# Seven block products in ten more pairs of tiles: the second halves of both gates and the output projection in 1024-column groups

## The chip, the cores and the metric

One NeuronCore of a Trainium2 chip runs the whole program. The metric is the device time of one execution in microseconds (us). A kernel is given by the median of its runs; a profiled execution also has a trace, and the trace's span is a little shorter than the time of the execution it belongs to.

## The reference

One layer (DEPTH 1) on 256 positions of width 2048, float32. Cut to what matters here:

```python
def mixer_block(x, g_norm, w_in, ln_g, ln_b, w_s, b_s, rpb, w_branch, w_out):
    h = rms_norm(x, g_norm)
    proj = h @ w_in                                   # 2048 -> 9216 columns
    uv, qkv, gates = jnp.split(proj, [2 * GM_WIDTH, 2 * GM_WIDTH + 3 * NA_WIDTH], axis=-1)
    q, k, v = jnp.split(qkv, 3, axis=-1)
    y_a = gmlp_branch(uv, ln_g, ln_b, w_s, b_s)       # 256 x 1024
    y_b = neighbourhood_attn(q, k, v, rpb)            # 256 x 1024
    g_a, g_b = jnp.split(jax.nn.sigmoid(gates), 2, axis=-1)   # 2048 columns each
    merged = g_a * (y_a @ w_branch[:GM_WIDTH]) + g_b * (y_b @ w_branch[GM_WIDTH:])
    return x + merged @ w_out                         # 2048 -> 2048

def conv_ffn(x, g_norm, w_up, conv_k, conv_b, w_down):
    up = rms_norm(x, g_norm) @ w_up                   # 2048 -> 2 * 5504
    ...                                               # depthwise convolution of width 3
    return x + (jax.nn.silu(gate) * val) @ w_down     # 5504 -> 2048
```

A final RMSNorm follows. Nearly all of the arithmetic is in the five matrix products with `w_in`, `w_branch`, `w_out`, `w_up` and `w_down`.

## The kernel before, in words

Every float32 operand of a matrix product is split into a high part of type fp32r and the low remainder, and each product is three matmuls: high by high, low by high, high by low (`three_products`, L365, its matmuls L368 to L370). The activations are split once; the weights are split as they arrive.

**The stream of weights.** `weight_stream` (L54) lists all products as groups of pieces of 128 x 1024 numbers (512 KB). The order of this list is the order of the program. For each piece `begin` (L340) first issues loads on the SP queue (`load`, L217; five raw buffers `wraw`), then prepares pieces up to four ahead (`prepare`, L336): ScalarE (ACT) writes the high part (`high`, L249), VectorE (DVE) the low part (`low`, L252) into a pair of tiles called a unit (`whi`, `wlo`). There are four units, and two more from the output projection on. Then the tasks that earlier steps put down for this piece run (`at`, `run_tasks`), and then TensorE (PE) gets the piece's matmuls. All engines work through their own queue in the order of the program.

**The kinds of group.** A `nat` group (`nat_step`, L394) has 512 output columns; a piece holds two input tiles of 128, and for each of the two blocks of 128 positions there are 2 x 3 matmuls into that block's PSUM bank: 12 matmuls a piece. The gates are four such groups of eight pieces for each half of the columns: `("gate", br, j)` for branch `br` 0 or 1 and column block `j` 0 to 3. The branch projections `("branch", br, j)` have four pieces each, the output projection `("out", j)` eight. A `ws` group keeps the weights in place (`u`, `q`, `k`, `up`). A `wide` group has 1024 output columns and one input tile a piece: 2 x 2 output blocks of 128 positions by 512 columns, 12 matmuls a piece, in four PSUM banks. The down projection is made of four wide groups (`wide_step`, L428).

**Seven block products.** In some pairs of neighbouring tiles of the down projection (`FF_SEVEN`) the 2 x 2 by 2 x 2 block product is done with seven block products in place of eight, in the manner of Strassen and Winograd. Such a pair takes 21 matmuls in place of 24 and uses seven banks, with the fourth output block eight, which is all of PSUM. For it the weights are prepared in three steps (`sums`, L286): `plain` splits one half block (the tile `half`) and one whole piece, `summed` makes four sums of 128 x 512 on DVE (L305 to L308) in the raw buffers and splits the first, `last` splits the second. That takes a half tile and three units for two pieces. The activations need four sums as well (`token_sums`). After the group's last such pair `combine` (L459) adds the extra banks to the output: ACT copies one bank (L464), DVE does the rest (L466, L467, and `rest`, L962), and the banks become free.

**Around the change.** The order is now: attention and the first gates; `branch` 0 and 1 for `j` 0 and 1; then for `j` 2 and 3 `gate(0, j)`, `gate(1, j)`, `branch(0, j)`, `branch(1, j)`; then `out` 0 to 3; then the first up group. `ev_gate` (L904) applies the sigmoid on ACT straight from PSUM. `ev_branch` (L913) multiplies the projection by its gate (L917) and adds the two branches (L921). `turn_m` (L925) transposes merged columns on PE (L935, eight transposes) two pieces later and splits them into the tiles `m` (L598, L603). `ev_out` (L971) adds the projection to `x2` (L968) and squares it on ACT; `turn_x2` (L988) transposes the result for the up projection (L995, L605). `open_x2` (L1232) gives the memory of the merge stage to `x2`, to the two more units and to the half tile, and loads `x` again on the POOL queue (L1239).

Of the kernel before, what the change touches and what calls it, by code (L numbers as in the profile page):

```python
# [48 lines left out]
FF_BLOCKS = ((0, 22), (22, 43))  # L49
FF_SEVEN = ((3, 5, 7), (2, 4, 6))  # L50
LAST = 4


def weight_stream():  # L54

    groups, order = {}, []

    def add(key, kind, w, pieces):
        groups[key] = (kind, w, pieces)
        order.extend([key] * len(pieces))
# [12 lines left out]

    def gate(br, j):  # L80
        nat(("gate", br, j), "w_in", 0, KD, (GA0, GB0)[br] + j * 512)

    def branch(br, j):
        nat(("branch", br, j), "w_branch", br * 8, 8, j * 512)

    add(("vg",), "wide", "w_in", [([k], (("x", T), (V0, 1024))) for k in range(KD)])
    for j in range(2):
        add(("u", j), "ws", "w_in", by_two(0, KD, (U0 + j * 512, 512)))
    for j in range(2):
        nat(("va", j), "w_in", 0, KD, VA0 + j * 512)  # L90
        qk(j)
    gate(0, 0)
    qk(2)
    gate(1, 0)
    qk(3)
    gate(0, 1)
    gate(1, 1)
    for j in range(2):
        branch(0, j)
        branch(1, j)  # L100
    for j in (2, 3):
        gate(0, j)
        gate(1, j)
        branch(0, j)
        branch(1, j)
    for j in range(4):
        nat(("out", j), "w_out", 0, KD, j * 512)
    for n, (f0, f1) in enumerate(FF_BLOCKS):
        for f in range(f0, f1, 2):
            nb = min(2, f1 - f) * 128  # L110
            add(("up", f), "ws", "w_up", by_two(0, KD, (f * 128, nb), (DFF + f * 128, nb)))
        for j in range(2):
            wide(("down", n, j), "w_down", j * 1024, down_tiles(n))
    return groups, order
# [38 lines left out]
def trunk_kernel(ctx, tc, x, weights, vectors, ln_g, ln_b, w_s_turned, b_s, rpb, norm_final, out):  # L153
# [46 lines left out]
    start_free = []  # L200
    unit_free = [(wpool, n) for n in range(UNITS[0])]
    half_free = []
    raw, units, halves = {}, {}, {}
    n_loaded = [0]
    tasks = {}
    preload = {}
# [31 lines left out]
    def unit(key, low_at=0):  # L238
# [3 lines left out]
        units[key] = (h, l, slot)  # L242
        return h, l

    def unit_done(key):
        unit_free.append(units.pop(key)[2])

    def high(h, w):
        nc.scalar.activation(h, w, AF.Copy)  # L249
# [175 lines left out]
                done(box["ps"], i + 1)  # L425
        return step

    def wide_step(key, acts, sevens, rest, done, by_block=0):  # L428


        n0, size = starts[key], size_of[key]
# [26 lines left out]

        def combine(i):  # L459

            nu, nv = (fx["p"].tile([128, 512], F32, name=f"comb{n}") for n in range(2))

            def one():
                nc.scalar.activation(nu, p(1), AF.Copy)  # L464
                rest(0, 0, nu, OP.add)
                nc.vector.tensor_sub(nu, nu, p(6))  # L466
                nc.vector.tensor_sub(nv, nu, p(7))  # L467
                free(p(1), p(6), p(7))

            def two():  # L470
                rest(0, 1, nu, OP.subtract)
                rest(0, 1, p(5), OP.add)
                rest(1, 0, nv, OP.add)

            def three():
                rest(1, 1, nv, OP.subtract)
                rest(1, 1, p(5), OP.add)
                free(p(5))

            for n, f in enumerate((one, two, three)):  # L480
                at(i + 3 if by_block else i + 1 + n, f)

# [420 lines left out]

    def ev_gate(br, j):  # L904
        def done(ps, i):
            g = mg["p"].tile([128, NT, 512], F32, name=f"g{br}", bufs=2)
# [3 lines left out]
            mg[br, j] = g  # L910
        return done

    def ev_branch(br, j):  # L913
        def done(ps, i):
            g = mg[br, j]
            for t in range(NT):
                nc.vector.tensor_mul(g[:, t, :], ps[t], g[:, t, :])  # L917
            free(*ps)
            if br == 1:
                for t in range(NT):  # L920
                    nc.vector.tensor_add(g[:, t, :], g[:, t, :], mg[0, j][:, t, :])  # L921
                at(i + 2, lambda: turn_m(j))
        return done

    def turn_m(j):  # L925
        if j == 0:
            mg["mp"], mg["m_st"] = pool("mT", "left")
            mg["mT"] = [mg["mp"].tile([128, 2, T], F32R, name=f"m{k}") for k in range(KD)]
        g = mg[1, j]
        for k2 in range(2):  # L930
            p = bank()
            for kk in range(2):
                c = k2 * 2 + kk
                for t in range(NT):
                    nc.tensor.transpose(p[:, kk * T + t * 128:kk * T + (t + 1) * 128],  # L935
                                        g[:, t, c * 128:(c + 1) * 128], ident)
            k = j * 4 + k2 * 2
            split_pair(p, mg["mT"][k:k + 2], None)
            free(p)

    def token_sums(f, s):

# [11 lines left out]


    rs = {}
    fx = {}

    def into_x2(j):
        def go(t, c, v, op):  # L960
# [20 lines left out]

    def norm2():
# [169 lines left out]
    for j in range(4):  # L1152
        steps["qk", j] = ws_step(("qk", j), xt, ev_qk(j))
        for br in range(2):
            steps["gate", br, j] = nat_step(("gate", br, j), xt, ev_gate(br, j))
            steps["branch", br, j] = nat_step(("branch", br, j), lambda k, br=br: yT[br * 8 + k], ev_branch(br, j))
    for n in range(len(FF_BLOCKS)):
# [3 lines left out]
    for j in range(4):  # L1161
        steps["out", j] = nat_step(("out", j), lambda k: mg["mT"][k], ev_out(j))
# [62 lines left out]
    def close_attention():  # L1225
        assert at_pool["done"] == HEADS // 2
        at_pool["st"].close()

    before["branch", 0, 1] = close_attention
    rs["ss"] = const.tile([128, NT, 4], F32, name="ss_2")  # L1230

    def open_x2():  # L1232
# [4 lines left out]
        rs["x2"] = xp.tile([128, NT, D], F32, name="x2")  # L1237
        for t in range(NT):
            nc.gpsimd.dma_start(rs["x2"][:, t, :], x[0, t * 128:(t + 1) * 128, :])  # L1239
        fx["p"], f_st = pool("seven", "right")  # L1240
        ctx.push(f_st)
        unit_free.extend((fx["p"], UNITS[0] + n) for n in range(UNITS[1]))
        half_free.extend((fx["p"], n) for n in range(HALVES))

    at(starts["out", 0] + 3, open_x2)

    def open_ff():
        mg["m_st"].close()
# [68 lines left out]
```

## Time and profile before

| | |
|---|---|
| median of three runs | 1321.99 us (1321.98 to 1323.04) |
| profiled execution | 1321.85 us, its span 1319.4 us |
| granted PE clock, mean | 0.997 |
| busy, PE / PE weight load / DVE / ACT / POOL | 1307.8 / 1114.7 / 945.5 / 728.8 / 100.1 us |
| branch 0 and 1, `j` = 1 | 356 to 378 us of the span |
| gates and branches, `j` = 2 and 3 | 378 to 511.6 us |
| output projection | 511.6 to 602.2 us |
| second part of the down projection, first group | 1198.5 to 1255 us |

The busy time of a group is the time in which at least one of its instructions ran. The matmuls are pipelined, so that the mean duration of one is longer than the distance from one to the next. A page of the profile gives shares over the whole span; the stretches in the table are the ones in which the changed work lies, or in which work of the same kind is done already.

### The profile page before, as it was taken

Reading aid. Unit: us, or ns where it says so; the run is one execution under the profiler, and the core shown is the slowest. Engines: PE = TensorE matmul, PEld = TensorE weight load, DVE = VectorE, ACT = ScalarE, POOL = GpSimd, SP = SyncE. Lnnn points to the kernel's source line nnn. Section 1 sums busy time; section 2 is a strip of 40 time slices with the busy share of each in tenths; the row PEclk is TensorE's granted clock in tenths of the full one; section 3 lists DMA queues with packets and bytes.
Section 4 is the critical chain, followed back from the end, with each engine's and each line's share of the span. In section 5 each row is a group of like instructions: output and inputs, shape, how many; then the busy total and the mean of one; then the engine's idle time right before and its main releaser. Section 6 shows DMA issues by size and latency. Waiting matters only on the chain.

```text
span 1319.4 us, 18485 instructions
## 1 busy us (share of the span) xinstructions
PE 1307.8 (99%) x6782; PEld 1114.7 (84%) x6782; DVE 945.5 (72%) x1362; ACT 728.8 (55%) x1072; POOL 100.1 (8%) x192
## 2 busy tenths in 40 slices
PE   9999999999999999999999999999999999999996
PEld 8888888888888888888888888888888888888885
DVE  6676667776564546565878777797858787869987
ACT  6755566676444444544655555554545555546553
POOL 0502075430000000000000000000000000000000
PEclk9999999999999999999999999999999999999998
DMA  9957676645556667665565656556655655546643
GB/s 349 316 170 213 202 207 196 202 156 184 188 188 187 194 188 259 196 201 182 179 203 176 196 178 202 178 169 229 209 190 191 192 187 197 180 140 223 235 164 128
DMA packets 74042, 261.40 MB, mean 198 GB/s; under 512 B 9568, under 2 KB 10720, under 8 KB 73440
## 3 DMA queue, kind: packets, MB, share of 16 engines
q1 hardware_dynamic: 69984, 252.46, 58.4%
q0 software_dynamic: 3680, 7.30, 2.1%
q8 instruction: 53, 0.87, 0.3%
q10 hardware_dynamic: 288, 0.47, 0.1%
q14 instruction: 37, 0.30, 0.1%
HBM read 256.00 MB, written 2.10 MB: 196 GB/s over the span
## 4 chain that ended last, share of the span: by engine, by line
PE 97%; DVE 2%; DMA 1%; ACT 0%; issue 0%; POOL 0%; DVEq 0%; ACTq 0%; POOLq 0%
PE bank L353 31%; PE bank L359 16%; PE bank L368 15%; PE bank L370 15%; PE bank L369 15%; PE bank L386 1%; PE bank L385 1%; PE bank L388 1%; DMA wraw<-in_weights_dram 1%; PE bank L834 1%; DVE wlo L252 0%; PE bank L886 0%; DVE x L962 0%; PE bank L565 0%; PE bank L708 0%; PE bank L995 0%
## 5 line engine op out<-in xcount | busy, mean ns | idle before, releaser
L252 DVE TENSOR_TENSOR wlo<-wraw,whi 128x1024 fp32r<-128x1024 f32 (+1 forms) x466 | 561.1, 1218 | 227.7 <-ACT whi L249 220.4
L249 ACT ACTIVATE whi<-wraw 128x1024 fp32r<-128x1024 f32 (+1 forms) x466 | 481.3, 1047 | 279.7 <-PE bank L369 162.4
L353 PE MATMUL bank<-h,whi 128*128 128x512 f32 x1760 | 426.2, 393 | 0.0
L353 PEld LDWEIGHTS bank<-h,whi 128*128 128x128 f32 x1760 | 321.7, 188 | 64.3
L359 PEld LDWEIGHTS bank<-h,wlo 128*128 128x128 f32 x1760 | 224.5, 188 | 9.8
L359 PE MATMUL bank<-h,wlo 128*128 128x256 f32 x1760 | 228.4, 281 | 0.0
L368 PE MATMUL bank<-whi,h 128*128 128x512 f32 x320 | 126.0, 394 | 0.0
L370 PE MATMUL bank<-wlo,h 128*128 128x512 f32 x320 | 124.7, 390 | 0.0
L369 PE MATMUL bank<-whi,h 128*128 128x512 f32 x320 | 124.6, 389 | 0.0
L370 PE MATMUL bank<-wlo,a 128*128 128x512 f32 x248 | 96.6, 389 | 0.0
L368 PE MATMUL bank<-whi,a 128*128 128x512 f32 x248 | 96.5, 389 | 0.0
L369 PE MATMUL bank<-whi,a 128*128 128x512 f32 x248 | 96.5, 389 | 0.0
L1024 ACT ACTIVATE tc<-ta,vec 128x256 f32<-128x256 f32 x86 | 47.0, 594 | 84.4 <-DVE ta L1022 84.4
L700 DVE TENSOR_TENSOR ta<-bank,tb 128x256 f32<-128x256 f32 x110 | 39.0, 417 | 67.1 <-ACT tb L698 67.1
L698 ACT ACTIVATE tb<-bank 128x256 f32<-128x256 f32 x110 | 36.2, 384 | 90.5 <-PE bank L353 85.7
L370 PEld LDWEIGHTS bank<-wlo,h 128*128 128x128 f32 x320 | 60.0, 188 | 12.7
L368 PEld LDWEIGHTS bank<-whi,h 128*128 128x128 f32 x320 | 60.1, 188 | 12.3
L369 PEld LDWEIGHTS bank<-whi,h 128*128 128x128 f32 x320 | 60.1, 188 | 12.0
L370 PEld LDWEIGHTS bank<-wlo,a 128*128 128x128 f32 x248 | 46.5, 188 | 9.9 <-DVE wlo L252 0.3
L369 PEld LDWEIGHTS bank<-whi,a 128*128 128x128 f32 x248 | 46.6, 188 | 9.7
L368 PEld LDWEIGHTS bank<-whi,a 128*128 128x128 f32 x248 | 46.6, 188 | 9.6
L1264 POOL DMA_DIRECT2D h<-in_norm_final_dram x4 | 2.2, 539 | 677.5 <-DVE wlo L252 676.9
(182 smaller groups left out, 1459.5 us busy)
## 6 DMA issues: line engine op xcount, KB each, us to landing
wraw<-in_weights_dram SPq DMA_DIRECT2D x446, 512.0 KB, 4.3
start<-in_weights_dram SPq DMA_DIRECT2D x13, 640.0 KB, 5.4
xs<-in_x_dram SPq DMA_DIRECT2D x2, 1024.0 KB, 8.9
vw<-va POOLq DMA_DIRECT2D x32, 64.0 KB, 5.9
x<-in_x_dram POOLq DMA_DIRECT2D x2, 1024.0 KB, 11.1
wraw<-in_weights_dram SPq DMA_DIRECT2D x8, 256.0 KB, 2.7
run<-in_rpb_dram POOLq DMA_DIRECT2D x64, 31.2 KB, 4.4
out_dram<-x SPq DMA_DIRECT2D x5, 256.0 KB, 2.9
```

The source lines that it names most:

```text
L249: nc.scalar.activation(h, w, AF.Copy)
L252: nc.vector.tensor_sub(l, w, h.bitcast(F32))
L353: nc.tensor.matmul(p, h[:, c:c + 128], acts(2 * n + k), start=n == 0 and k == 0, stop=last and k == tiles - 1)
L359: nc.tensor.matmul(p[:, :T], l[:, c:c + 128], acts(2 * n + k)[:, 0, :], start=False, stop=False)
L368: nc.tensor.matmul(p, xh, wh, start=start, stop=False)
L369: nc.tensor.matmul(p, xl, wh, start=False, stop=False)
L370: nc.tensor.matmul(p, xh, wl, start=False, stop=stop)
L385: nc.tensor.matmul(p, xh, h[:, cs], start=n == 0, stop=False)
L386: nc.tensor.matmul(p, xl, h[:, cs], start=False, stop=False)
L698: nc.scalar.activation(t, p[:, T:], AF.Copy)
L700: nc.vector.tensor_add(a, p[:, :T], t)
L1024: nc.scalar.activation(v, u, AF.Identity, scale=ck[:, 1, ch:ch + 1], bias=ck[:, 3, ch:ch + 1])
```

## The change

- The gates of the columns 1024 to 2047 of each branch become one wide group, `("gates", 0)` and `("gates", 1)`, which stand one after the other ahead of the last four branch groups. The output projection becomes two wide groups `("out", 0)` and `("out", 1)`.
- Seven block products are used in the pairs 2, 4 and 6 of both gate groups and in the pairs 3 and 5 of both output groups, ten pairs in all.
- The gate groups have nothing to add to, so `combine` gets a second form (`fresh`): one copy on ACT and four subtractions on DVE write the four blocks of the gate tile. `ev_gates` then adds the bank of each block (DVE) and applies the sigmoid in place (ACT).
- The activations' sums for the gates are made by `x_sums` from the parts in `xT`, three sets which both groups share, while the branch groups of `j` = 1 run. Those for the output are made in `turn_m`.
- While the gate groups run, a pool in the memory that the attention has left gives two more units, the half tile, the sums and a scratch tile; `fewer_units` and `close_gates` take it back, and the tiles `m` follow it there.
- All of PSUM is in use in a gate group. So `turn_m(0)` and `turn_m(1)` move behind the gates, to the pieces 4 and 7 after the start of `branch(0, 2)`, and the tiles of branch 1's gates get four buffers in place of two. `turn_m(3)` and `open_x2` come one piece earlier, `turn_x2` at the pieces 3 and 5 of the second output group and at the pieces 2 and 4 of the first up group.

```diff
+GATE_SEVEN = ((2, 4, 6), (2, 4, 6))
+OUT_SEVEN = ((3, 5), (3, 5))
+TURN_M = (4, 7, 2, 1)
+TURN_X2 = ((3, 5), (2, 4))
...
+    for br in range(2):
+        wide(("gates", br), "w_in", (GA0, GB0)[br] + 1024, range(KD))
     for j in (2, 3):
-        gate(0, j)
-        gate(1, j)
         branch(0, j)
         branch(1, j)
-    for j in range(4):
-        nat(("out", j), "w_out", 0, KD, j * 512)
+    for j in range(2):
+        wide(("out", j), "w_out", j * 1024, range(KD))
...
     def unit_done(key):
-        unit_free.append(units.pop(key)[2])
+        slot = units.pop(key)[2]
+        if slot[0] not in gone:
+            unit_free.append(slot)
+
+    def more_units(p):
+        fx["p"] = p
+        unit_free.extend((p, UNITS[0] + n) for n in range(UNITS[1]))
+        half_free.extend((p, n) for n in range(HALVES))
+
+    def fewer_units():
+        gone.append(fx["p"])
+        for free_list in (unit_free, half_free):
+            free_list[:] = [slot for slot in free_list if slot[0] is not fx["p"]]
...
+            def one_fresh():
+                nc.scalar.activation(fresh(0, 0), p(1), AF.Copy)
+                nc.vector.tensor_sub(nu, fresh(0, 0), p(6))
+                nc.vector.tensor_sub(fresh(1, 0), nu, p(7))
+                free(p(1), p(6), p(7))
+
+            def two_fresh():
+                nc.vector.tensor_sub(fresh(0, 1), p(5), nu)
+                nc.vector.tensor_sub(fresh(1, 1), p(5), fresh(1, 0))
+                free(p(5))
+
+            if fresh:
+                at(i + 1, one_fresh)
+                at(i + 2, two_fresh)
+                return
...
+    def ev_gates(br):
+        def done(p, t, c, i):
+            g = gates_tile(br)(t, c)
+            nc.vector.tensor_add(g, p, g)
+            nc.scalar.activation(g, g, AF.Sigmoid, scale=st1["r"][:, t:t + 1])
         return done
...
-                at(i + 2, lambda: turn_m(j))
+                if j > 1:
+                    at(i + TURN_M[j], lambda: turn_m(j))
...
+            if any(k // 2 in o for o in OUT_SEVEN):
+                f = mg["mp"].tile([128, 4, 128], F32, name="sums", bufs=2)
+                nc.scalar.activation(f, p.rearrange("p (a t) -> p a t", a=4), AF.Copy)
+                mg["s", k] = sums_in_place(f, mg["mp"].tile([128, 2, 4, 128], F32R, name=f"s{k}"), cur[0] + 1)
...
+    def x_sums(k):
+        f = fx["p"].tile([128, 4, 128], F32, name="sums")
+        for n in range(2):
+            a = xT[k + n].bitcast(F32)
+            nc.vector.tensor_add(f[:, 2 * n:2 * n + 2], *(a[:, e, :].rearrange("p (a t) -> p a t", a=2) for e in range(2)))
+        mg["x", k] = sums_in_place(f, fx["p"].tile([128, 2, 4, 128], F32R, name=f"s{k}"), cur[0])
+
+    def sums_in_place(f, z, i):
+
+        def make():
+            nc.vector.tensor_sub(f[:, 3, :], f[:, 1, :], f[:, 3, :])
+            nc.vector.tensor_sub(f[:, 1, :], f[:, 1, :], f[:, 0, :])
+            nc.vector.tensor_sub(f[:, 0, :], f[:, 0, :], f[:, 3, :])
+            nc.vector.tensor_sub(f[:, 2, :], f[:, 2, :], f[:, 0, :])
+            nc.scalar.activation(z[:, 0], f, AF.Copy)
+
+        at(i, make)
+        at(i + 1, lambda: nc.vector.tensor_sub(z[:, 1], f, z[:, 0].bitcast(F32)))
+        return [(z[:, 0, n, :], z[:, 1, n, :]) for n in (3, 0, 1, 2)]
...
     def ev_out(j):
-        def done(ps, i):
-            for t in range(NT):
-                v = add_rest(ps[t], t, j)
-                nc.scalar.activation(junk, v, AF.Square, accum_out=rs["ss"][:, t, j:j + 1])
-            free(*ps)
-            at(i + 2, lambda: turn_x2(j))
-            if j == 3:
-                at(i + 2, norm2)
+        def done(p, t, c, i):
+            q = 2 * j + c
+            v = add_rest(p, t, q)
+            nc.scalar.activation(junk, v, AF.Square, accum_out=rs["ss"][:, t, q:q + 1])
+            if (t, c) == (1, 1):
+                for n in range(2):
+                    at(i + TURN_X2[j][n], lambda n=n: turn_x2(2 * j + n))
+                if j == 1:
+                    at(i + 2, norm2)
         return done
...
     def close_attention():
         assert at_pool["done"] == HEADS // 2
         at_pool["st"].close()
+        p, mg["x_st"] = pool("gates", "left")
+        more_units(p)
+        for n, k in enumerate(sorted({2 * p for g in GATE_SEVEN for p in g})):
+            at(cur[0] + 2 + 2 * n, lambda k=k: x_sums(k))
+
+    def close_gates():
+        mg["x_st"].close()
+
+    at(starts["gates", 1] + 2 * max(GATE_SEVEN[1]) + 1, fewer_units)
+    at(starts["branch", 0, 2] + 3, close_gates)
+    for j in range(2):
+        at(starts["branch", 0, 2] + TURN_M[j], lambda j=j: turn_m(j))
...
-    at(starts["out", 0] + 3, open_x2)
+        more_units(p)
+
+    at(starts["out", 0] + 2, open_x2)
```

More of the change, by code (lines that the diff above doesn't have):

```diff
@@ L202, in trunk_kernel @@
     half_free = []
-    raw, units, halves = {}, {}, {}
+    raw, units, halves, fx = {}, {}, {}, {}
     n_loaded = [0]
@@ L243, in unit @@
         return h, l
+    gone = []
     def unit_done(key):
-        unit_free.append(units.pop(key)[2])
+        slot = units.pop(key)[2]
[9 more added lines that the diff above has]
+            free_list[:] = [slot for slot in free_list if slot[0] is not fx["p"]]
     def high(h, w):
@@ L426, in ws_step, with wide_step @@
         return step
-    def wide_step(key, acts, sevens, rest, done, by_block=0):
+    def wide_step(key, acts, sevens, rest, done, by_block=0, fresh=None):
         n0, size = starts[key], size_of[key]
@@ L459, in combine @@
         def combine(i):
-            nu, nv = (fx["p"].tile([128, 512], F32, name=f"comb{n}") for n in range(2))
+            nu = fx["p"].tile([128, 512], F32, name="comb0")
+            nv = None if fresh else fx["p"].tile([128, 512], F32, name="comb1")
             def one():
@@ L905, in done @@
         def done(ps, i):
-            g = mg["p"].tile([128, NT, 512], F32, name=f"g{br}", bufs=2)
+            g = mg["p"].tile([128, NT, 512], F32, name=f"g{br}", bufs=2 + 2 * br)
             for t in range(NT):
@@ L910, in done, with gates_tile, fresh @@
             mg[br, j] = g
+        return done
+    def gates_tile(br):
+        def fresh(t, c):
+            if (br, 2 + c) not in mg:
+                mg[br, 2 + c] = mg["p"].tile([128, NT, 512], F32, name=f"g{br}", bufs=2 + 2 * br)
+            return mg[br, 2 + c][:, t, :]
+        return fresh
+    def ev_gates(br):
[3 more added lines that the diff above has]
+            nc.scalar.activation(g, g, AF.Sigmoid, scale=st1["r"][:, t:t + 1])
         return done
@@ L956, in trunk_kernel @@
     rs = {}
-    fx = {}
     def into_x2(j):
@@ L1154, in trunk_kernel @@
         for br in range(2):
-            steps["gate", br, j] = nat_step(("gate", br, j), xt, ev_gate(br, j))
+            if j < 2:
+                steps["gate", br, j] = nat_step(("gate", br, j), xt, ev_gate(br, j))
             steps["branch", br, j] = nat_step(("branch", br, j), lambda k, br=br: yT[br * 8 + k], ev_branch(br, j))
+    for j in range(2):
+        seven.update({starts["gates", j] + 2 * p: p for p in GATE_SEVEN[j]})
+        seven.update({starts["out", j] + 2 * p: p for p in OUT_SEVEN[j]})
+        steps["gates", j] = wide_step(("gates", j), of_tiles(xt), lambda k: mg["x", k], None,
+                                      ev_gates(j), fresh=gates_tile(j))
+        steps["out", j] = wide_step(("out", j), of_tiles(lambda k: mg["mT"][k]), lambda k: mg["s", k],
+                                    into_x2(j), ev_out(j))
     for n in range(len(FF_BLOCKS)):
@@ L1160, in trunk_kernel @@
             seven.update({starts[key] + 2 * p: p for p in FF_SEVEN[n]})
-    for j in range(4):
-        steps["out", j] = nat_step(("out", j), lambda k: mg["mT"][k], ev_out(j))
     for n, (f0, f1) in enumerate(FF_BLOCKS):
@@ L1227, in close_attention @@
         at_pool["st"].close()
+        p, mg["x_st"] = pool("gates", "left")
[6 more added lines that the diff above has]
+    at(starts["branch", 0, 2] + 3, close_gates)
+    for j in range(2):
+        at(starts["branch", 0, 2] + TURN_M[j], lambda j=j: turn_m(j))
     before["branch", 0, 1] = close_attention
@@ L1239, in open_x2 @@
             nc.gpsimd.dma_start(rs["x2"][:, t, :], x[0, t * 128:(t + 1) * 128, :])
-        fx["p"], f_st = pool("seven", "right")
+        p, f_st = pool("seven", "right")
         ctx.push(f_st)
-        unit_free.extend((fx["p"], UNITS[0] + n) for n in range(UNITS[1]))
-        half_free.extend((fx["p"], n) for n in range(HALVES))
-    at(starts["out", 0] + 3, open_x2)
+        more_units(p)
+    at(starts["out", 0] + 2, open_x2)
     def open_ff():
```

## The prediction

> **What bounds the kernel now.** I read the page first, its busy times and the chain of waits, then the timeline of PE, then the groups of instructions with shapes kept apart, and last the windows of the stretches that the change touches.
>
> ```profile
> span 1319.4 us, 18485 instructions
> PE 1307.8 (99%) x6782; PEld 1114.7 (84%) x6782; DVE 945.5 (72%) x1362; ACT 728.8 (55%) x1072; POOL 100.1 (8%) x192
> PE 97%; DVE 2%; DMA 1%; ACT 0%; issue 0%; POOL 0%; DVEq 0%; ACTq 0%; POOLq 0%
> ...
> 445.46 0.39 PE L368 MATMUL bank<-whi,h 128*128 128x512 f32 x1
> ...
> 450.67 0.39 PE L370 MATMUL bank<-wlo,h 128*128 128x512 f32 x1
> ...
> L370 PEld LDWEIGHTS bank<-wlo,a 128*128 128x128 f32 x248 | 46.5, 188 | 9.9 <-DVE wlo L252 0.3
> ```
>
> PE is busy for 1307.8 of 1319.4 us, and 97% of the chain that ended last is PE. Busy matmuls alone would prove little, since they overlap: the row says 0.39 us, but the 24 matmuls of two gate pieces start from 445.46 to 450.67, so one starts every 5.21 / 23 = 0.2265 us. That spacing is the price of a matmul here. In the last row the weight loads waited 0.3 us in all for a split weight, in a stage that already has seven block products. So the kernel is PE from end to end, and a matmul taken out is worth its spacing as long as no other engine comes late.
>
> **The change part by part.**
>
> *Matmuls removed.* Before: four gate groups of 8 pieces x 12, 384, and as many in the output. After: a gate group has ten single tiles x 12 and three pairs x 21, 183, two of them 366; an output group has twelve x 12 and two x 21, 186, two of them 372. That is 18 + 12 = 30 fewer. 30 x 0.2265 = 6.80 us off the path. The 64 transposes only change places. The Trainium skill has a rule that would make this smaller: "TensorE: Matmul & The Clock Gate", section Back-to-back issue gap, gives a sustained 131 ns for a matmul of 512 columns in a stream of weight loads and matmuls; by it the 30 would be worth 3.9 us. The measured 0.2265 us disagrees, and the measurement decides.
>
> *Weights on DVE and ACT.* Ten pairs go from two splits to the long preparation.
>
> ```profile
> L252 DVE TENSOR_TENSOR wlo<-wraw,whi 128x1024 fp32r<-128x1024 f32 x458 | 555.7, 1227 | 225.7 <-ACT whi L249 218.4 <-PE bank L935 6.0
> L249 ACT ACTIVATE whi<-wraw 128x1024 fp32r<-128x1024 f32 x458 | 476.4, 1054 | 277.6 <-PE bank L369 162.4 <-PE bank L353 45.6 <-DVE wraw L306 26.5
> L252 DVE TENSOR_TENSOR half_lo<-wraw,half_hi 128x512 fp32r<-128x512 f32 x12 | 8.2, 685 | 2.3 <-ACT half_hi L249 2.3
> L306 DVE TENSOR_TENSOR wraw<-wraw,wraw 128x512 f32<-128x512 f32 x12 | 8.3, 692 | 0.4
> L466 DVE TENSOR_TENSOR comb<-comb,bank 128x512 f32<-128x512 f32 x4 | 2.8, 689 | 0.3
> L945 DVE TENSOR_TENSOR sums<-full,sums 128x128 f32<-128x128 f32 x6 | 1.8, 292 | 0.2
> 356.00:378.00 22.00, 22.00 (x103) 18.31 (x102) 14.18 (x19) 9.58 (x12) 0.00 (x0) 1.00 0.58 177
> 378.00:602.20 224.20, 224.20 (x1015) 186.19 (x1014) 123.11 (x129) 102.29 (x126) 1.13 (x2) 1.00 0.63 203
> 1198.50:1255.00 56.50, 56.50 (x250) 46.55 (x249) 52.58 (x66) 32.02 (x39) 0.00 (x0) 1.00 0.67 225
> ```
>
> A window row gives the stretch, then the busy time of PE, weight load, DVE, ACT and POOL. On DVE a plain pair costs 2 x 1.227 = 2.45 us, a seven-product pair 0.685 + 3 x 1.227 + 4 x 0.692 = 7.13: 4.68 more, 46.8 for ten. The rest by the 0.69 of a 128 x 512 operation: `combine` 4 in each gate group and 8 in each output group, 24 x 0.69 = 16.6; eight additions in `ev_gates`, 5.5; the sums in `turn_m` twice 4 x 0.292 + 0.685, 3.7; one transposed block that comes in from before 378, 1.4. Together 74 us into 378 to 602.2, where DVE is busy 123.1: 197 of the 217.4 us that remain, 91%. The three `x_sums` (two additions of 256 columns at the 0.42 that rows of that width show, and 4 x 0.292 + 0.685, 2.7 each) put 8.1 into 356 to 378 and one `turn_m` of 1.4 leaves: 20.9 of 22. ACT gets 0.62 + 1.05 = 1.7 more a pair and some 5 for the rest, 124 of 217: it stays free. All of it costs nothing while it lies beside PE, and the cover exists already: from 1198.5 to 1255 DVE was busy 93% of the time on the same pattern (pairs 2, 4, 6) and PE had no pause. Once the cover is gone, DVE's excess falls on PE one for one.
>
> I walked DVE's queue through a gate group with these durations. The branch's multiplications and additions occupy it for the first 3 us; each pair's preparation ends two to four us before PE wants it; a second group of 39 us of DVE work (ten splits, three pairs, 2.8 for `combine`, 2.8 for the additions) stands against 183 x 0.2265 = 41.4 us of PE. Price taken: nothing.
>
> *Waits of the raw buffers.* A pair's second raw piece can only be loaded when the previous pair's first sum has been split, five pieces earlier.
>
> ```profile
> wraw<-in_weights_dram SPq DMA_DIRECT2D x446, 512.0 KB, 4.3
> 1277.17 3.57 DMA wraw<-in_weights_dram
> ...
> 1290.60 5.25 DMA wraw<-in_weights_dram
> ...
> 1239.25 1.23 DVE L252 TENSOR_TENSOR wlo<-wraw,whi 128x1024 fp32r<-128x1024 f32 x1 [1.23 <-ACT whi L249]
> 1240.39 0.69 DVE L962 TENSOR_TENSOR x<-x,comb 128x512 f32<-128x512 f32 x1
> ...
> 1241.90 0.69 DVE L467 TENSOR_TENSOR comb<-comb,bank 128x512 f32<-128x512 f32 x1
> 1242.51 1.22 DVE L252 TENSOR_TENSOR wlo<-wraw,whi 128x1024 fp32r<-128x1024 f32 x1
> ...
> 1247.42 0.69 DVE L962 TENSOR_TENSOR x<-x,bank 128x512 f32<-128x512 f32 x1
> ...
> 1198.50 0.39 PE L368 MATMUL bank<-whi,a 128*128 128x512 f32 x1
> 1234.73 0.39 PE L368 MATMUL bank<-whi,a 128*128 128x512 f32 x1
> ```
>
> Round this ring: landing 4.3, ACT 1.05, DVE 1.23, four sums 2.77, split 1.23, 10.6 us, against 45 x 0.2265 = 10.2 us of PE for a pair of each kind. It loses 0.4 a turn, twice in a gate group and once in an output group, out of a lead of about 3 us: nothing.
>
> *Hand-over of the banks.* A group now takes all eight banks, and the next group opens with four that `combine` frees. In a gate group only two pieces, 5.4 us, lie between the last seven-product pair and the next group; its four first blocks then follow every 0.68 us, so the last bank is wanted 7.5 us after that pair. In an output group it is four pieces, and 12.9 us. The nearest row is the down projection: the pair ends at 1234.73, the second subtraction at 1242.6 (7.9 us later), the last addition at 1248.1 (13.4). Taken over, the first gate group would have its last bank after the split at 1242.51 and two more operations, less the one addition that a gate group does not have: 9.7 against 7.5, 2.2 us of pause; into the branch group 0; first to second output group 13.4 against 12.9, 0.5; into the up group, which opens four banks within 0.7 us, 13.4 against 11.6, 1.8. Upper end 4.5 us, lower end 0. The down group starts under 5.4 us of convolution work on DVE, a gate group under 2.8, and an output group has one such pair fewer; so I stand near the lower end and take 0.2 us.
>
> *Moved steps.* `turn_m(3)` comes one piece earlier.
>
> ```profile
> 512.44 1.29 DVE L921 TENSOR_TENSOR g<-g,g 128x512 f32<-128x512 f32 x2
> ...
> 517.08 1.03 PE L935 MATMUL bank<-ident,g 128*128 128x128 f32 x8
> 512.09 1.13 POOL L1239 DMA_DIRECT2D x<-in_x_dram  x2 [226.74 <-DVE g L917]
> ```
>
> The merged block was ready at 513.7 and the transposes came at 517.1; one piece earlier is 514.4, still after it: 0. The two loads of `x` on POOL stand earlier in the program too, but they waited for DVE to release the gates' memory, not for their place; POOL has nothing behind them, and the first use is now 30 us after. The weight loads on SP keep number, size and order. `turn_m(0)` and `turn_m(1)` hide in the branch groups as before; no matmul needs their tiles before the output. The last `turn_x2` comes two pieces, over 10 us, ahead of the up piece that reads it. The wait for the attention's memory finds it free: its last product lies two pieces earlier.
>
> *Sum.* Span 1319.4 - 6.80 + 0.2 = 1312.8. The profiled execution took 1321.85, 2.45 over its span, which the change does not touch: 1315.25. The median of the runs, 1321.99, is 0.14 above the profiled execution, hence 1315.4 us.
>
> **The rivals.**
>
> *The banks come late.* As priced, up to 4.5 us of pauses at the four hand-overs: 1315.2 + 4.5 = 1319.7. For it: the 7.9 and 13.4 us of the down group. Against: DVE enters the new groups with less work in front of it. Halfway, 1317.5, is as likely as the whole.
>
> *The ring of raw buffers becomes the bound, and the kernel is slower.* If a landing takes L in place of 4.3 us, each turn loses L - 3.9. With 3 us of lead a group, the two gate groups pause 2 x (2(L - 3.9) - 3) and the output groups 2 x ((L - 3.9) - 3). The gain is gone at L = 7.1, and at 7.5 the kernel is 2.6 us slower; L = 8 gives 1315.2 + 12.6 = 1327.8. For it: the output stage shares the DMA engines with the load of `x`. Against: landings of 3.6 and 5.3 us in the rows above, where the same ring ran, with a DMA share of 0.67 against 0.63.
>
> *The matmuls are worth less than their spacing.* By the 0.39 us row they would be worth more, 11.7 us, and overlap excludes that. If instead PE had pauses that the rows hide, a shorter spacing would be left; bounded by the weight load of 0.188 us below which no pair can go, 30 x 0.188 = 5.6, so 1316.5. By the Trainium skill's 131 ns it would be 1318.1 us; that case lies inside the same small chance.
>
> **How the numbers follow.** The forecast (under 1 us of pauses) 0.71; late banks 0.16, a little over half of it still faster; the ring 0.05, most of it slower; matmuls worth less 0.04; small pauses at places not named 0.04. A measurement of this kernel can tell about 0.2%, 2.6 us. Faster needs less than 1319.3: 0.86; within 0.2% 0.10; slower 0.04. The range goes from 1314.6 (no pause, 0.6 for the runs' own spread) to 1318.8, where most of the late banks lie inside.
>
> **What would show it.** The page of the changed kernel should count 6752 matmuls and a PE busy time near 1301; PE should have no pause between the first gate group and the first up group over 0.3 us; DVE busy about 1026 us; the window of gates and output about 217 us long with DVE near 91%. Wrong would be: PE rows that wait for a bank at a group's start (late banks), ACT splits that wait over 3 us for `wraw` in the new groups (the ring), weight loads that wait for `wlo`, or a span that falls by 3.9 and not by 6.6.

## The result, and the profile after

The changed kernel takes 1315.12 us, the median of six runs (1314.72 to 1316.12), against 1322.14 us for the kernel before in the same comparison (1321.8 to 1323.14). The ratio is 0.9946, with a 95% interval of 0.9933 to 0.9959: 7.0 us faster. The profiled execution took 1315.79 us, its span 1313.6.

The head of the page, its busy times and the chain of waits of the changed kernel, and after them the row of its weight loads among the DMA issues:

```profile
span 1313.6 us, 18614 instructions
PE 1302.2 (99%) x6752; PEld 1109.9 (84%) x6752; DVE 1015.1 (77%) x1485; ACT 746.9 (57%) x1103; POOL 99.5 (8%) x192
PE 92%; DMA 3%; DVE 3%; ACT 1%; issue 1%; POOL 0%; DVEq 0%; ACTq 0%; POOLq 0%
...
wraw<-in_weights_dram SPq DMA_DIRECT2D x446, 512.0 KB, 4.4
```

Thirty matmuls fewer, PE busy 5.6 us less, DVE busy 69.6 us more; a weight piece lands after 4.4 us in place of 4.3. PE's share of the chain fell from 97% to 92%: the chain now runs through other engines in places, but from the first branch group on PE is busy all the same, as the windows below show. A better measure than the span is the stretch from the first matmul of the first branch group to the last matmul of the program, since the start of an execution varies (last section). The windows of that stretch, before and then after; the columns are the length, then the busy time of PE, weight load, DVE, ACT and POOL, the granted clock, the DMA share and GB/s:

```profile
334.03:1308.79 974.76, 974.76 (x4985) 831.32 (x4983) 710.65 (x989) 510.32 (x705) 5.88 (x8) 1.00 0.59 191
```

```profile
335.58:1303.52 967.94, 967.94 (x4954) 825.54 (x4953) 781.05 (x1114) 528.91 (x737) 5.87 (x8) 1.00 0.59 192
```

It is 6.82 us shorter, and PE is busy through all of it, both times. The prediction had 6.80 for the matmuls.

The waits of PE in the changed kernel, all of them (total, times, longest, in us):

```profile
PE bank L599 <- POOL ident masks.py:199: 1.4, 1, 1.4
PE bank L377 <- DVE wlo L270: 0.3, 1, 0.3
```

The first is at the start of the program, the second at 81.7 us in the second `u` group. The stretch with the new groups has none.

### The profile page after: what moved, and what is told of

Same layout as the page of the kernel before. It is cut to its first block, busy times and chain, and to the rows that moved or that the text cites. A ratio compares the mean times of both kernels' runs of the same rounds, so it can differ in the third digit from the quotient of the medians.

```text
span 1313.6 us, 18614 instructions
## 1 busy us (share of the span) xinstructions
PE 1302.2 (99%) x6752; PEld 1109.9 (84%) x6752; DVE 1015.1 (77%) x1485; ACT 746.9 (57%) x1103; POOL 99.5 (8%) x192
## 4 chain that ended last, share of the span: by engine, by line
PE 92%; DMA 3%; DVE 3%; ACT 1%; issue 1%; POOL 0%; DVEq 0%; ACTq 0%; POOLq 0%
PE bank L371 29%; PE bank L377 15%; PE bank L386 15%; PE bank L388 15%; PE bank L387 15%; DMA wraw<-in_weights_dram 2%; DMA start<-in_weights_dram 1%; DVE wlo L270 1%; ACT whi L267 1%; PE bank L868 1%; PE bank L920 0%; PE bank L599 0%; PE bank L404 0%; PE bank L403 0%; DVE x L1034 0%
## 5 line engine op out<-in xcount | busy, mean ns | idle before, releaser
L270 DVE TENSOR_TENSOR wlo<-wraw,whi 128x1024 fp32r<-128x1024 f32 (+1 forms) x476 | 571.0, 1216 | 158.6 <-ACT whi L267 154.4
L267 ACT ACTIVATE whi<-wraw 128x1024 fp32r<-128x1024 f32 (+1 forms) x476 | 489.0, 1046 | 240.8 <-PE bank L387 76.3
L377 PEld LDWEIGHTS bank<-h,wlo 128*128 128x128 f32 x1760 | 224.5, 188 | 10.3 <-DVE wlo L270 0.5
L386 PE MATMUL bank<-whi,h 128*128 128x512 f32 x284 | 111.8, 394 | 0.0
L388 PE MATMUL bank<-wlo,h 128*128 128x512 f32 x284 | 110.7, 390 | 0.0
L387 PE MATMUL bank<-whi,h 128*128 128x512 f32 x284 | 110.6, 389 | 0.0
L388 PEld LDWEIGHTS bank<-wlo,h 128*128 128x128 f32 x284 | 53.3, 188 | 11.3
L386 PEld LDWEIGHTS bank<-whi,h 128*128 128x128 f32 x284 | 53.3, 188 | 11.0
L387 PEld LDWEIGHTS bank<-whi,h 128*128 128x128 f32 x284 | 53.4, 188 | 10.7
```

The costliest lines, as they stand in the source:

```text
L270: nc.vector.tensor_sub(l, w, h.bitcast(F32))
L377: nc.tensor.matmul(p[:, :T], l[:, c:c + 128], acts(2 * n + k)[:, 0, :], start=False, stop=False)
L386: nc.tensor.matmul(p, xh, wh, start=start, stop=False)
L387: nc.tensor.matmul(p, xl, wh, start=False, stop=False)
L388: nc.tensor.matmul(p, xh, wl, start=False, stop=stop)
```

## The experiments

**Theory:** the gain is the number of matmuls times their spacing, and all added work on DVE and ACT hides. **First rival:** part of it comes from the new grouping itself. **Second rival:** more would be gained if DVE or the banks did not hold PE up somewhere. From the third run on there was a third question, of the last two down groups; it is told there.

### The new groups without seven block products

```diff
-GATE_SEVEN = ((2, 4, 6), (2, 4, 6))
-OUT_SEVEN = ((3, 5), (3, 5))
+GATE_SEVEN = ((), ())
+OUT_SEVEN = ((), ())
...
-            nc.vector.tensor_add(g, p, g)
-            nc.scalar.activation(g, g, AF.Sigmoid, scale=st1["r"][:, t:t + 1])
+            nc.scalar.activation(g, p, AF.Sigmoid, scale=st1["r"][:, t:t + 1])
```

> The changed kernel without any seven-product pair in the gates and the output; the 1024-column groups, the order, the extra units and the later transposes stay; the gates' sigmoid is taken straight from PSUM again. Theory 1 (the gain is the 30 matmuls at 0.2265 us each, all else lies beside PE): 6782 matmuls again and 1322.0 us, within 0.7 us of the kernel before. Rival A (the larger groups, the more units or the moved transposes bring part of the gain): below 1320.5 us. The start of the up group should lie 0.8 us earlier than before in the trace, since one of four blocks of transposes has moved behind it, and nothing more.

Measured: 1321.86 us (11 runs), ratio 1.0 (0.9991 to 1.0009). The windows from the first matmul of the gates to the output, and from there to the up groups, first of this kernel and then of the changed one:

```profile
379.00:512.24 133.24, 133.24 (x601) 110.59 (x600) 68.25 (x71) 57.00 (x67) 0.00 (x0) 1.00 0.59 182
512.24:601.96 89.72, 89.72 (x409) 74.55 (x408) 51.18 (x56) 42.41 (x56) 1.13 (x2) 1.00 0.69 223
```

```profile
379.94:509.12 129.18, 129.18 (x583) 107.15 (x582) 109.85 (x137) 69.92 (x88) 0.00 (x0) 1.00 0.57 192
509.12:596.12 87.00, 87.00 (x397) 72.30 (x396) 76.94 (x95) 48.17 (x64) 1.13 (x2) 1.00 0.66 231
```

Between the two pairs of rows lies the gain and nothing else: 18 matmuls and 4.06 us in the first stretch, 12 and 2.72 in the second, 0.226 and 0.227 us for each. Every later stage is the same length in both within 0.1 us. DVE is busy 67.4 us more in the two stretches and PE shows none of it. Against the kernel before, the regrouped kernel starts its up groups 0.89 us earlier after the first branch matmul (267.32 us in place of 268.21), as expected, and its up groups take 0.89 us longer: a block of transposes has moved. The first rival falls.

### The gates alone, the output alone

```diff
-OUT_SEVEN = ((3, 5), (3, 5))
+OUT_SEVEN = ((), ())
```

> Seven products in the gates only, six pairs; the output groups have none. Theory 1: 18 matmuls fewer, 18 x 0.2265 = 4.1 us: 1318.0 us. Rival A: if the regrouping paid, more than 4.1 us. Rival B (DVE's added work costs something in the gates): less than 3.5 us.

Measured: 1317.65 us (5 runs), ratio 0.9966 (0.9953 to 0.9978), 4.5 us faster than before; the stage from the gates to the output takes 129.16 us, as in the changed kernel. As the theory said.

The other half is the first experiment's edit with `OUT_SEVEN` left as the change has it.

> Seven products in the output only, four pairs; the gates' sigmoid straight from PSUM. Theory 1: 12 matmuls fewer, 2.7 us: 1319.3 us; together with the gates alone the two gains add to 6.8 us. Rival B: less than 2.2 us.

Measured: 1320.94 us (11 runs), ratio 0.9991 (0.9982 to 0.9999): 1.2 us faster where 2.7 were expected. The output stage itself did its part:

```profile
512.50:599.50 87.00, 87.00 (x398) 72.30 (x397) 77.17 (x96) 48.40 (x65) 1.13 (x2) 1.00 0.67 231
1196.64:1308.14 111.50, 110.78 (x486) 90.81 (x485) 98.22 (x123) 60.62 (x78) 2.59 (x2) 1.00 0.53 181
```

87.00 is the changed kernel's number. But the last two groups of the down projection, 600 us further on and untouched by any edit, take 111.50 us in place of the 110.29 of before and the 110.25 of the changed kernel. There the split on ACT waited for a weight piece. First the row of this kernel, then one microsecond of its DMA queues (1265.64 to 1266.64 us; packets, MB, share of 16 engines), then the same split in the changed kernel:

```profile
1270.40 1.06 ACT L267 ACTIVATE whi<-wraw 128x1024 fp32r<-128x1024 f32 x1 [2.95 <-DMA wraw<-in_weights_dram]
```

```profile
q1 hardware_dynamic: 12, 0.05, 27.3%
q8 instruction: 1, 0.02, 10.3%
```

```profile
1265.51 1.06 ACT L267 ACTIVATE whi<-wraw 128x1024 fp32r<-128x1024 f32 x1 [1.23 <-DMA wraw<-in_weights_dram]
```

A wait of 2.95 in place of 1.23 us, and PE then waits for `wlo` in the same group, at one place 0.85 us by the distance of its matmuls. Beside the landing that is late, a fetch of 16 KB of instructions stands on the queue q8. It begins 1.6 us after the first of a series of four weight loads is issued (1265.05), and that load lands after 5.33 us; in the changed kernel the fetch comes 5.6 us after the start of such a series, when the first load has landed, after 3.62 us. In these groups a fetch comes about every 29 us, and its place against the weight stream is not the same in every kernel. This was a new theory, that the fetch delays the weights; the runs with shifted instructions below test it.

### The four sums left out

```diff
-            nc.vector.tensor_add(r0[:, c0], r0[:, c0], r0[:, c1])
-            ...
+            if pieces[i][0][0] == "down":
+                nc.vector.tensor_add(r0[:, c0], r0[:, c0], r0[:, c1])
+                ...
```

> The changed kernel with the four sums of weights left out in the ten new pairs, 40 DVE operations of 0.69 us, 27.7 us of DVE work; the splits and the matmuls stay, so that the gates and the output are computed from wrong weights. Theory 1: the sums are hidden, 1315.1 us within 0.5 us, PE as before and DVE with about 28 us less. Rival B (DVE is close enough to the bound to hold PE up): 1 us or more faster.

Measured: 1315.3 us (5 runs), ratio 0.9946 (0.9932 to 0.996), and the two stages 129.17 and 86.99 us; DVE is busy 989.8 us in place of 1015.1. Twenty-five microseconds of DVE work go and PE does not notice: the sums hide to the last one, and the second rival has nothing left to gain in the kernel as it is.

### The banks released later

Six operations of 128 x 512 on a scratch tile ahead of `one_fresh` in the first gate group:

```diff
             def one_fresh():
+                if key == ("gates", 0):
+                    for _ in range(6):
+                        nc.vector.tensor_sub(junk, junk, junk)
```

> The changed kernel with six more DVE operations of 128 x 512 on a scratch tile right ahead of the first gate group's combination, some 3.7 us, so that its banks come free that much later. In the trace of the changed kernel the last of these banks is free at 423.3 us and wanted at 423.5. Theory 1 with its hand-over of the banks: PE pauses about 3.5 us at the start of the second gate group, and 1318.6 us in all. Rival (the lead of the prepared weights swallows it): no pause, 1315.1 us.

Measured: 1319.84 us (10 runs), ratio 0.9984 (0.9975 to 0.9993), 4.7 us above the changed kernel where 3.5 were expected; its stage is 4.98 us longer. The hand-over in the changed kernel, on DVE and then the first matmul of the second gate group on PE:

```profile
418.41 1.23 DVE L270 TENSOR_TENSOR wlo<-wraw,whi 128x1024 fp32r<-128x1024 f32 x1 [1.25 <-ACT whi L267]
419.55 0.68 DVE L501 TENSOR_TENSOR comb<-g,bank 128x512 f32<-128x512 f32 x1
420.26 0.69 DVE L502 TENSOR_TENSOR g<-comb,bank 128x512 f32<-128x512 f32 x1
420.87 1.22 DVE L270 TENSOR_TENSOR wlo<-wraw,whi 128x1024 fp32r<-128x1024 f32 x1
422.00 0.68 DVE L506 TENSOR_TENSOR g<-bank,comb 128x512 f32<-128x512 f32 x1
422.61 0.68 DVE L507 TENSOR_TENSOR g<-bank,g 128x512 f32<-128x512 f32 x1
...
421.42 0.39 PE L386 MATMUL bank<-whi,h 128*128 128x512 f32 x1
```

L507 is the last reader of the last bank and ends at 423.29. The group's fourth block begins nine matmuls after 421.42, at 423.46. So 0.17 us are left. The same place with the six operations, on DVE and in PE's waits:

```profile
419.35 4.32 DVE L502 TENSOR_TENSOR junk<-junk 128x512 f32<-128x512 f32 x6
423.58 0.68 DVE L504 TENSOR_TENSOR comb<-g,bank 128x512 f32<-128x512 f32 x1
```

```profile
PE bank L386 <- DVE comb L504: 3.0, 1, 3.0
PE bank L386 <- DVE g L510: 1.4, 1, 1.4
```

The operations took 4.32 us, not 6 x 0.61 = 3.7: each depends on the one before it, and they then follow every 0.72 us. DVE also came to the place 0.77 us later here (419.35 - 378.97 = 40.38 us after the gates' first matmul, against 419.55 - 379.94 = 39.61). Less the margin of 0.17 that makes 4.9, and the stage grew by 4.98: what DVE is late at this place falls on PE whole, as pauses at two banks in turn.

### More work on DVE

One operation of 128 x 512 (on the scratch tile) behind every second split of a gate piece, then behind every one:

```diff
-                queue.append((i, 1, 0, split_piece(i)))
+                queue.append((i, 1, 0, with_load(i, split_piece(i))))
...
+    def with_load(i, f):
+        if pieces[i][0][0] != "gates" or i % 2:
+            return f
+        def go():
+            f()
+            nc.vector.tensor_sub(junk, junk, junk)
+        return go
```

> The changed kernel with one more DVE operation of 128 x 512 on a scratch tile for every second piece of the two gate groups, 16 operations, about 10.4 us of DVE work where DVE is idle for 7.7 of 83.0 us. Theory 1 (DVE work costs nothing until its idle time and lead are used up): between 0 and 3 us, 1316.5 us. Rival B (DVE holds PE up already): 8 to 10 us, 1324 us.

> The same for every piece of the two gate groups, 32 operations, about 20.8 us. Theory 1: past the point, one for one: 20.8 less 7.7 of idle time and some 4 of lead, 9 to 13 us, 1326 us. Rival (the lead of the units and the idle time of the stages after swallow it): under 3 us.

Measured: with 16 operations 1318.8 us (8 runs), ratio 0.9973 (0.9963 to 0.9983), 3.7 us above the changed kernel, more than the 0 to 3 that were expected; with 32 1327.7 us (4 runs), ratio 1.0043 (1.003 to 1.0057), slower than before the change. The gate-to-output windows of the two:

```profile
379.63:512.17 132.54, 130.23 (x583) 106.85 (x582) 118.06 (x152) 70.47 (x89) 0.00 (x0) 1.00 0.57 187
```

```profile
378.70:520.34 141.64, 134.68 (x583) 108.20 (x582) 127.69 (x168) 70.93 (x89) 0.00 (x0) 0.98 0.55 175
```

With 16, DVE is busy 118.06 of 132.54 us and yet the stage has grown by 3.36. PE's two pauses stand at the hand-over of the banks, 1.11 and 1.53 us by the distances of its matmuls. On DVE no idle time is left there, from 407.6 to beyond 428 us; some rows of its queue:

```profile
414.53 0.68 DVE L349 TENSOR_TENSOR junk<-junk 128x512 f32<-128x512 f32 x1
415.13 1.22 DVE L270 TENSOR_TENSOR wlo<-wraw,whi 128x1024 fp32r<-128x1024 f32 x1
...
422.01 0.69 DVE L349 TENSOR_TENSOR junk<-junk 128x512 f32<-128x512 f32 x1
422.61 0.69 DVE L511 TENSOR_TENSOR comb<-g,bank 128x512 f32<-128x512 f32 x1
...
425.67 0.68 DVE L517 TENSOR_TENSOR g<-bank,g 128x512 f32<-128x512 f32 x1
```

The subtractions begin at 422.61, which is 42.98 us after the gates' first matmul (379.63). In the changed kernel they begin at 419.55, 39.61 us after it (379.94). That is 3.37 us later, and the stage lost about as much: 2.9 us at the two pauses, with the slower matmul behind each, and 0.5 in small delays ahead of them. With 32 operations PE also waits seven times for the low part of a weight, 3.9 us in all, and runs at half speed for a time (last section). DVE's idle time in the groups cannot be drawn on: in the changed kernel's window from the gates to the up groups it stands ahead of the splits, and ends with ACT:

```profile
L270 DVE TENSOR_TENSOR wlo<-wraw,whi 128x1024 fp32r<-128x1024 f32 x92 | 110.4, 1221 | 25.6 <-ACT whi L267 22.6 <-PE bank L984 1.5 <-PE bank L387 0.3
```

If the second two subtractions were what costs, an earlier place for them must win part of it back under the same load:

```diff
-                at(i + 2, two_fresh)
+                at(i + 1, two_fresh)
```

> The kernel with 16 more DVE operations in the gate groups (1318.8 us), with the second step of the gates' combination put right behind the first, ahead of the next piece's split. There PE paused 1.1 us for the bank that the first step frees and 1.5 us for the one that the second frees. Theory 1 with the hand-over of the banks: the last bank comes 1.2 us sooner, the second pause falls to about 0.3 us, 1317.6 us. Rival (the pauses are weights that come late): no change, or worse by the later split.

Measured: 1318.26 us (5 runs), ratio 0.997 (0.9958 to 0.9983). The second pause goes from 1.53 to 0.40 us, as expected, the stage only from 132.54 to 131.86, and the median by 0.5, which lies inside the two intervals. The distances of PE's matmuls show the rest. The first pause, 1.1 us, is untouched by this edit; the 0.5 us ahead of it are there as before; and 0.4 of the 1.1 us that were won come back as delays in the second gate group (448.9 to 459.7 us), which the kernel with 16 operations does not have. Why they come there the runs don't show. The hand-over of the banks carries most of the loss, not all of it.

### More pairs

```diff
-GATE_SEVEN = ((2, 4, 6), (2, 4, 6))
-OUT_SEVEN = ((3, 5), (3, 5))
+GATE_SEVEN = ((1, 2, 4, 6), (1, 2, 4, 6))
+OUT_SEVEN = ((2, 4, 6), (2, 4, 6))
```

> Seven products in more pairs: 1, 2, 4 and 6 of both gate groups and 2, 4 and 6 of both output groups, 14 in place of 10; 12 more matmuls fewer, 2.7 us of PE. DVE gets 4 x 4.68 us more for the weights and some 4.6 for the activations: in the gate groups about 84.7 us of work against 81.6 of PE, in the output groups about 86 to 88 against 85.7. Theory 1 (the cover ends where DVE's work passes PE's): the gain is eaten in the gates and about held in the output, 1315 us, between 1312.4 (all hidden) and 1318. A rival by which DVE never matters: 1312.4 us.

Measured: 1346.96 us (5 runs), ratio 1.0186 (1.0172 to 1.02). Twelve matmuls fewer, and 32 us slower. The longest of PE's waits:

```profile
PE bank L386 <- DVE g L507: 5.4, 1, 5.4
PE bank L386 <- DVE h L639: 4.8, 1, 4.8
PE bank L1068 <- DVE h L639: 2.9, 1, 2.9
PE bank L386 <- DVE x L1040: 2.7, 1, 2.7
PE bank L386 <- DVE g L965: 2.5, 1, 2.5
PE bank L388 <- DVE wlo L270: 2.3, 4, 0.8
```

All but the last are waits for a bank, and the five make 18.3 us. An early pair wants the extra banks while the evictions of the group before it still hold them (L965, L1040); in the second output group the transposes of `x2` and a pair want the same banks (L639, 7.7 us in all); and the first gate group's last pair hands its banks over late (L507). Waits for weights and half speed after the pauses (last section) make up part of the rest. The expectation counted DVE's time and not the banks. One pair more at a place where no bank is short:

```diff
-OUT_SEVEN = ((3, 5), (3, 5))
+OUT_SEVEN = ((3, 4, 5), (3, 5))
```

> The changed kernel with the pairs 3, 4 and 5 in the first output group, where the last bank is free 5 us before it is wanted: 3 matmuls fewer, 0.68 us, for 4.7 us of DVE in that group and 1.9 in the branch groups. Theory 1 with the hand-over: the lag is covered, no pause above 0.3 us, 1314.4 us. Rival (three pairs in a row outrun the preparation, which takes 7.1 us for a pair that PE does in 4.8): pauses of 1 to 4 us, 1316 us or more.

Measured: 1320.88 us (11 runs), ratio 0.999 (0.9981 to 0.9999): the rival was right. Three pairs in a row give ACT and DVE no plain pair to recover in: ACT starts the first summed piece of the three at 525.11, 532.68 and 539.55, 7.6 and 6.9 us apart, where PE's 21 matmuls take 4.8. And the extra sums in `turn_m` make DVE late for the last merged columns. PE's waits, and the spacing behind the last two:

```profile
PE bank L984 <- DVE g L969: 1.4, 2, 1.1
...
PE bank L386 <- ACT whi L267: 0.8, 1, 0.8
PE bank L388 <- DVE wlo L270: 0.8, 1, 0.8
```

```profile
543.17 0.63 PE L388 MATMUL bank<-wlo,s 128*128 128x512 f32 x1
543.59 0.63 PE L386 MATMUL bank<-whi,s 128*128 128x512 f32 x1
```

No version was found that beats the changed kernel.

### The instruction fetch

The first of these two kernels is the output alone with 18 transposes added into an unused part of a bank early in the first up group, the second the changed kernel with 22; both shift the fetches against the weight stream and change no instruction of the last groups.

```diff
         p = bank()
+        if name == "rb2":
+            for _ in range(18):
+                nc.tensor.transpose(p[:, 256:384], ident, ident)
```

> The output-only kernel (1320.9 us, 1.5 us more than its 12 matmuls give) with 18 more transposes of the identity into an unused part of a bank early in the first up group: 18 x 0.1 = 1.8 us and 36 PE instructions. In the output-only kernel the last down group took 111.5 us in place of 110.2: one weight piece landed 1.5 us late, while a 16 KB fetch of instructions ran for 1.65 us beside it, 69 us after the start of the second part of the down projection; in kernels where the fetch falls at 65 or at 72 to 74 the group takes 110.2. The fetch should come 36 instructions, about 4 us, earlier. Theory F (the fetch delays the landing): the last group is 110.2 us again, 1321.4 us in all. Rival (something in this kernel's buffers or order makes it late): 111.5 us still, 1322.7 us.

> The changed kernel with 22 such transposes, 2.2 us and 44 PE instructions, so that its fetch moves from 74 us to 69 us after that start. Theory F: its last group grows from 110.25 to about 111.5 us, 1318.6 us in all. Rival: 110.25 us and 1317.3 us.

Measured for the output alone: the last two down groups take 110.33 us again (111.50 without the shift), and ACT's wait is 1.25. In the changed kernel they take 112.26 (110.25 without), and the wait is there now:

```profile
1269.56 1.06 ACT L267 ACTIVATE whi<-wraw 128x1024 fp32r<-128x1024 f32 x1 [3.00 <-DMA wraw<-in_weights_dram]
```

The fetch that matters begins 70.0 and 71.0 us after the first matmul of these groups in the two kernels with the long wait. In the twelve other kernels it begins at 63 to 66 or at 72.4 to 74.8, and the groups take 110.1 to 110.4 us. The first load of the series is issued 68.0 to 68.9 us after that matmul in all fourteen. It lands after 5.3 and 5.4 us in the two kernels whose fetch begins while it is under way, and after 3.5 to 3.8 us in the others. So the delay follows the place of the fetch, in both directions. The place itself was forecast only roughly: the fetch moved by 6.8 us where 4 were expected, and by 3.2 where 5 were. How a fetch of 16 KB delays 512 KB by 1.5 us or more the runs don't show. In the second kernel 0.4 of the 2.0 us were lost ahead of the late piece (at 1263.6 us, where PE waited for a split), which this does not explain. The totals are 1322.36 (10 runs) and 1319.84 (10 runs), each about 1 us above what was expected. For the second, 0.75 us lie in the last groups and 0.2 in the transposes; for the first, whose profiled execution took 1321.54, where it lies was not settled.

## Why the prediction was right

**Matmuls.** 30 x 0.2265 = 6.80 us was the forecast, 4.06 + 2.72 = 6.78 came out of the two stages. The rival that a matmul is worth less than its spacing falls by the 0.226 us that each removed matmul gave. The 131 ns for 512 columns in the section Back-to-back issue gap of the Trainium skill's "TensorE: Matmul & The Clock Gate", 3.9 us for the thirty, do not agree with it. The rival's bound of 0.188 us was no bound either: in the `ws` groups of the kernel before, 1760 weight loads of 0.188 us by their rows (L359) are busy for only 224.5 us, 0.128 each, and their matmuls of 256 columns follow every 0.12 us (eight from 85.30 to 86.24).

**DVE and ACT at nothing.** Right for the path: without the sums the time is the same. The size was off: DVE 1026 us busy was forecast and 1015.1 came, and 86% of the window in place of 91%:

```profile
379.90:596.10 216.20, 216.20 (x979) 179.45 (x978) 186.77 (x231) 118.12 (x151) 1.13 (x2) 1.00 0.61 207
```

The step multiplied durations of rows, and neighbouring operations that don't depend on each other overlap: 422.00 + 0.68 is 0.07 past the next start, 420.87 + 1.22 is 0.09. The four sums of a pair, each of which needs the one before, do not: they follow every 0.72 us. Added up over the two traces, the durations of DVE's instructions grew by 78.8 us (1005.8 to 1084.6) and its busy time by 69.6. So 9.2 of the 10.9 us are overlap, and the other 1.7 are durations that were summed a little high. The sentence that the excess falls on PE only when the cover is gone was too easy as well: 16 small operations, some 10 us, cost 3.4 us with DVE 89% busy: its idle time lay at other places of the queue than the added work.

**The ring of raw buffers at nothing.** Right: landings of 4.4 us, and in the gate groups ACT waited at most 1.41 us for a piece. Its price for slow landings was not tried directly (and by its own formula the kernel is 2.8 us slower at 7.5 us, not 2.6); the one late piece of the output-alone kernel, 1.7 us more of a wait, cost 1.2 us.

**Banks at 0.2 us.** Right for the sum, since PE has no pause. It was right by less than it seemed. The prediction's reason was that DVE enters a gate group under 2.8 us of other work in place of 5.4; that takes 2.6 off the 9.7 of the down group's row, and 7.1 against the 7.5 wanted leaves no pause. In the first gate group the last bank came 7.3 us after the pair (415.98, 24 matmuls ahead of 421.42). So the reason held, but that no pause came at all is in part luck: in four kernels with the same gate groups that bank came 43.06, 43.19, 43.35 (the changed kernel) and 43.62 us after the gates' first matmul, and is wanted at 43.52; in the last of them, the one with one more pair, PE lost 0.3 us there. For the hand-over between the output groups the row had promised too much delay: DVE's last operation on a bank ends at 549.9, 8.6 us after the pair and not 13.4, and the bank is wanted at 554.2, 4.3 us later; into the up group the margin is 2.7. Only the first of the four is tight.

**The sum.** 1315.25 us for the profiled execution was forecast and 1315.79 measured, 1315.4 for the median and 1315.12 measured. The first difference does not come from the change: the profiled execution reached the first branch group 1.55 us later than the one of before (335.58 against 334.03), while the stretch from there on is 6.82 us shorter, where 6.80 less 0.2 was forecast. Behind the last matmul it took 0.5 us less, and outside the span 0.3 less.

## What to carry to other kernels

When one engine is busy from end to end, count what it no longer does at the spacing of its instructions, and look for the loss only at the places where it must be handed something: here a bank, with 0.17 us to spare. The busy share of the engine that prepares says little about what it can still take, as 10 us of added work in an engine that was idle 14% of the time showed; walk its queue from the last piece of a group to the first use in the next. And a change may move a stage that it does not touch: compare the stages one by one before the totals.

## What the runs showed of the hardware

**Half speed after short pauses.** After the 5.4 us pause of the kernel with more pairs the matmuls follow every 0.427 us until 440.00, and then every 0.227:

```profile
435.63 0.80 PE L386 MATMUL bank<-whi,h 128*128 128x512 f32 x1 [5.45 <-DVE g L507]
...
439.21 0.63 PE L388 MATMUL bank<-wlo,h 128*128 128x512 f32 x1
439.64 0.52 PE L386 MATMUL bank<-whi,h 128*128 128x512 f32 x1
440.00 0.40 PE L387 MATMUL bank<-whi,h 128*128 128x512 f32 x1
```

So a pause of 5.4 us costs some 2 us more (ten matmuls at 0.2 us extra). The granted clock is 0.50 from 433.07 to 439.89 us, so it fell during the pause, and 1.00 around it. The Trainium skill, "TensorE: Matmul & The Clock Gate", Part 1, tells of such a clock, halved after an idle window of about 3.4 us and full again after as long a busy one. The three stretches at 0.50 inside this kernel are 3.41, 6.83 and 10.24 us long, and one, two and three windows of that length agree with them. The length of the pause does not agree everywhere: with 32 operations the half speed came with a pause of 2.2 us (0.50 from 428.43 to 435.26), and in the kernel with one more pair with two of 0.9 us, at 540 and 542 (0.50 from 542.70 to 546.11), while a pause of 3.0 us in the kernel with late banks did not bring it.

**The start.** The half speed is seen at the start of an execution too. In the profiled execution of the changed kernel the first matmuls on weights follow every 0.43 us until 6.98; in that of before, the same program at that place, none does. The records of the granted clock begin, at full speed, at 7.16 and at 4.71 us. The seventh matmul on weights begins at 7.53 us against 6.53: 1.0 of the 1.55 us by which the changed kernel came later to the first branch group.

**The instruction fetch,** as shown above: when a fetch of 16 KB began while the first of four weight loads was under way, that load landed after 5.3 to 5.4 us in place of 3.5 to 3.8, and a stage that has nothing to do with the change took 1.2 to 2.0 us longer.
